# Feed-forward's first projection by seven block products in place of eight, with the sums of weight blocks made by accumulating transfers

## The chip, the cores and the metric

The kernel runs on one core of one Trainium2 chip. The metric is device time in microseconds of one execution; a lower number is better. A core has five engines with queues of their own, each worked off in order: TensorE (PE in the profile; its weight loads are PEld), VectorE (DVE), ScalarE (ACT), GpSimd (POOL) and SyncE (SP). Transfers between the chip's memory (HBM) and the core's memory (SBUF) are issued from one of these queues and carried by 16 DMA engines. TensorE writes its results into eight banks of PSUM.

## What is computed

The reference runs four layers over a sequence of 512 tokens of width 1024, all in 32-bit floats. Each layer is a mixer (an attention, a convolution module, a gated recurrence, another attention) and then a feed-forward, and every one of the four feed-forwards has the same shape:

```
def swiglu_ffn(h, w_ffn_in, w_ffn_out):
    g, u = jnp.split(h @ w_ffn_in, 2, axis=-1)
    return (jax.nn.silu(g) * u) @ w_ffn_out

def conv_ffn(x, w_up, conv_w, conv_b, w_down):
    gate, val = jnp.split(x @ w_up, 2, axis=-1)
    ...
    return (jax.nn.silu(conv) * val) @ w_down
```

`h` is 512x1024, `w_ffn_in` 1024x5632 and `w_ffn_out` 2816x1024. The first two feed-forwards are of the first kind. The last two put a causal convolution of width 3 over the gate ahead of the `silu`.

## The kernel before

**Matmuls in three passes.** Every 32-bit operand is split into a high part, rounded to the format that TensorE takes at full rate, and the low rest. ScalarE writes the high part (a copy), VectorE the low one (a subtraction). A product is then three matmuls (`mm3`): high by high, high by low, low by high. The activations lie in SBUF feature-major as `xh` and `xl`, eight blocks of 128 features by 512 tokens.

**Weights in units.** All weights are 379 units of 128x1024 (512 KB) in one tensor `wall`, in the order of use. `w_dma` loads unit after unit on SP's queue, `w_hi` (ScalarE) and `w_lo` (VectorE) split them, and `W.cur` counts the units taken by the matmuls. Loads run at most `AHEAD_DMA` = 8 units ahead of it, splits `AHEAD` = 5.

**The feed-forward.** `ffn` goes over 22 pairs of units (128 gate columns and the 128 value columns that go with them). For each unit `fm_unit` takes 8 blocks of 128 features by three matmuls of 512 columns: 24 matmuls, 48 for a pair. The first four units go by `fm_quads`, in halves of 256 columns: 256 tokens for all four units first, since the later tokens are not ready yet. `epi` follows each pair: `silu` (with the convolution in the last two feed-forwards) on the gate, the product with the value, and the split of that product into `p`. `out_proj` then takes the 22 units of the second projection, each by 8 groups of three matmuls of 512 columns, and as its results come, `boundary` runs residual, norm (whose power GpSimd takes in `rms_scale`), transposes (`xt`) and the split into `xh` and `xl` for the next stage, one block of 128 tokens (`tb`) after the other.

**Order.** A scheduler in Python (`Sched`), which runs when the program is built, sets the order of each engine's queue: tasks yield operations with an engine and an assumed cost, and the one that can start first is issued, with priorities to settle ties. That order is then fixed: an engine whose next instruction must wait holds up what stands behind it. Working memory is a pool of 34 slots of 128x1024 (`spool`), a pool of eight 128x512 tiles, and the eight PSUM banks.

## Time and profile before

| | |
|---|---|
| Three runs | 2326.4, 2327.54 and 2328.59 us; median 2327.54 |
| The profiled execution | 2326.68 us, of which the profile's span is 2324.9 |
| PE busy | 2306.1 us, 99% of the span |
| DVE, ACT, POOL busy | 1197.4 (52%), 912.1 (39%), 134.8 (6%) us |
| DMA | 224.68 MB in all, 97 GB/s on average; wall's queue 27.9% of the 16 engines |
| Granted TensorE clock | 0.998 of full speed |

The span runs from the first to the last instruction; the time of an execution is 1.78 us longer here. "Busy" of an engine is the time in which at least one of its instructions ran. Matmuls overlap in their records: each lasts longer than the distance to the next, so the distance from start to start, and not the duration, is what one costs in a stream. A granted clock of 1.00 means 2.4 GHz.

### The profile page before, as it was taken

To read this page: it belongs to the slowest core of one execution; us is meant where nothing else is said; L and a number is where in the kernel's file an instruction comes from. 1 tells how busy PE (TensorE), PEld (TensorE's weight loads), DVE (VectorE), ACT (ScalarE), POOL (GpSimd) and SP (SyncE) were. 2 spreads that over 40 slices of the span, in tenths; PEclk is the share of its full clock that TensorE was granted. 3 is DMA by queue.
4 is the path that set the end of the run, shared out by engine and by line. 5 is a ranking of instruction groups with operands and counts; after the bars stand their busy time and mean duration, and the time that the engine had idled before them with its cause. 6 is when DMAs were issued, how large, how long until landed. Compare 5 with 4: busy or idle time off the path is not lost.

```text
span 2324.9 us, 29594 instructions
## 1 busy us (share of the span) xinstructions
PE 2306.1 (99%) x11888; PEld 1969.2 (85%) x11888; DVE 1197.4 (52%) x2038; ACT 912.1 (39%) x1614; POOL 134.8 (6%) x162
## 2 busy tenths in 40 slices
PE   9999999999999999999999999999999999999998
PEld 9888988888978988888888888888888998888887
DVE  5786433333687633333564875444434655444432
ACT  6454323222466322323443444333322664333321
POOL 0000000000284000000000000000000000000000
PEclk9999999999999999999999999999999999999999
DMA  4223322233333222234121214222243022222340
GB/s 179 101 82 118 119 73 91 81 128 107 120 138 126 91 91 76 90 106 154 73 73 64 73 47 135 91 73 77 96 163 109 19 90 93 91 73 76 105 137 36
DMA packets 62936, 224.68 MB, mean 97 GB/s; under 512 B 6984, under 2 KB 7240, under 8 KB 62800
## 3 DMA queue, kind: packets, MB, share of 16 engines
q1 hardware_dynamic: 62368, 222.41, 27.9%
q8 instruction: 93, 1.52, 0.3%
q10 hardware_dynamic: 432, 0.40, 0.1%
q14 instruction: 43, 0.35, 0.0%
HBM read 220.67 MB, written 2.11 MB: 96 GB/s over the span
## 4 chain that ended last, share of the span: by engine, by line
PE 95%; POOL 1%; DVE 1%; ACT 1%; issue 1%; DMA 0%; SPq 0%; POOLq 0%; ACTq 0%
PE fm L539 18%; PE fm L540 18%; PE fm L541 18%; PE op L539 9%; PE op L541 9%; PE op L540 9%; PE tm L539 2%; PE tm L541 2%; PE tm L540 2%; POOL cy L1190 1%; PE xt L689 1%; PE O L1745 1%; PE S L1508 1%; PE o L1571 1%; PE PT L1734 1%
## 5 line engine op out<-in xcount | busy, mean ns | idle before, releaser
L539 PE MATMUL fm<-xh,wh 128*128 128x512 f32 (+1 forms) x2160 | 794.8, 368 | 0.0
L540 PE MATMUL fm<-xl,wh 128*128 128x512 f32 (+1 forms) x2160 | 787.3, 364 | 0.2 <-DVE xl L699 0.2
L541 PE MATMUL fm<-xh,wl 128*128 128x512 f32 (+1 forms) x2160 | 787.3, 364 | 0.0
L507 DVE TENSOR_TENSOR wl<-wr,wh 128x1024 fp32r<-128x1024 f32 x379 | 457.4, 1232 | 287.2 <-ACT wh L498 182.3
L498 ACT ACTIVATE wh<-wr 128x1024 fp32r<-128x1024 f32 x379 | 387.6, 1052 | 264.0 <-DMA wr<-wall 138.5
L541 PEld LDWEIGHTS fm<-xh,wl 128*128 128x128 f32 x2160 | 407.9, 189 | 65.3
L539 PEld LDWEIGHTS fm<-xh,wh 128*128 128x128 f32 x2160 | 408.3, 189 | 61.7
L540 PEld LDWEIGHTS fm<-xl,wh 128*128 128x128 f32 x2160 | 408.3, 189 | 61.4 <-DVE xl L699 0.4
L539 PE MATMUL op<-wh,p 128*128 128x512 f32 x704 | 274.9, 390 | 0.4 <-DVE sg L805 0.4
L541 PE MATMUL op<-wh,p 128*128 128x512 f32 x704 | 274.0, 389 | 0.0
L540 PE MATMUL op<-wl,p 128*128 128x512 f32 x704 | 273.9, 389 | 0.0
L805 DVE TENSOR_TENSOR sg<-fm,sg 128x512 f32<-128x512 f32 x88 | 60.9, 692 | 383.2 <-PE fm L541 376.1
L530 ACT ACTIVATE p<-sg 128x512 fp32r<-128x512 f32 x88 | 55.6, 632 | 357.4 <-DVE sg L805 357.4
L539 PEld LDWEIGHTS op<-wh,p 128*128 128x128 f32 x704 | 132.1, 188 | 28.1 <-DVE sg L805 0.9
L541 PEld LDWEIGHTS op<-wh,p 128*128 128x128 f32 x704 | 132.1, 188 | 27.7
L540 PEld LDWEIGHTS op<-wl,p 128*128 128x128 f32 x704 | 132.2, 188 | 27.0
L660 POOL TENSOR_TENSOR ss<-ss,mhalf 128x1 f32<-128x1 f32 x48 | 26.0, 541 | 1417.1 <-DVE ss L655 1417.0
L539 PE MATMUL op<-wh,y 128*128 128x512 f32 x256 | 102.7, 401 | 0.2 <-DVE y L1004 0.2
L541 PE MATMUL op<-wh,y 128*128 128x512 f32 x256 | 100.0, 391 | 0.0
L540 PE MATMUL op<-wl,y 128*128 128x512 f32 x256 | 99.8, 390 | 0.0
L531 DVE TENSOR_TENSOR p<-sg,p 128x512 fp32r<-128x512 f32 x88 | 60.9, 692 | 61.4 <-ACT p L530 61.4
L1190 POOL TENSOR_TENSOR cy<-cp,cy 128x512 f32<-128x512 f32 x60 | 86.1, 1434 | 30.2 <-ACT cp L1189 26.3
(247 smaller groups left out, 2269.9 us busy)
## 6 DMA issues: line engine op xcount, KB each, us to landing
wr<-wall SPq DMA_DIRECT2D x379, 512.0 KB, 3.6
row<-rows SPq DMA_DIRECT2D x14, 512.0 KB, 3.9
cm<-cmat SPq DMA_DIRECT2D x14, 512.0 KB, 4.0
h<-x SPq DMA_DIRECT2D x8, 256.0 KB, 6.6
nck<-negc SPq DMA_DIRECT2D x4, 512.0 KB, 5.1
alibi<-alibi SPq DMA_DIRECT2D x4, 512.0 KB, 4.4
out<-out SPq DMA_DIRECT2D x8, 256.0 KB, 2.1
mk<-masks SPq DMA_DIRECT2D x2, 288.0 KB, 5.3
```

What stands on the lines that cost most here:

```text
L498: yield act(1024, lambda: A.activation(out=b.t, in_=r.t, func=AF.Copy), (r,), (b,))
L507: yield dve(1024, lambda: V.tensor_tensor(out=b.t, in0=r.t, in1=hh.t.bitcast(F32), op=ALU.subtract), (r, hh), (b,))
L530: yield act(n, lambda: A.activation(out=y0, in_=raw, func=AF.Copy), (rb,), (yb,), psum=psum)
L531: yield dve(n, lambda: V.tensor_tensor(out=y1, in0=raw, in1=y0.bitcast(F32), op=ALU.subtract), (rb,), (yb,))
L539: T.matmul(out, lhsT=a[0], rhs=b[0], start=s, stop=False)
L540: T.matmul(out, lhsT=a[0], rhs=b[1], start=False, stop=False)
L541: T.matmul(out, lhsT=a[1], rhs=b[0], start=False, stop=e)
L660: yield Op("POOL", 0.29 + 0.167 * cols, lambda: G.tensor_tensor(out=ss[:, 8:8 + cols], in0=ss[:, 4:4 + cols], in1=mhalf[:, :cols], op=ALU. ...
L689: T.transpose(b[:, 128 * i:128 * i + 128], n[:, c:c + 128], ident)
L805: yield dve(512, lambda: V.tensor_tensor(out=c.t, in0=u.t, in1=c.t, op=ALU.mult), (u, c), (c,))
L1190: yield pool(512, lambda: G.tensor_tensor(out=y.t, in0=p.t, in1=y.t, op=ALU.add), (p,), (y,))
L1508: T.matmul(b[:, 128 * i:128 * i + 128].rearrange("p (j l) -> p j l", l=ln), lhsT=mix[:, 128 * i:128 * i + 128], rhs=dims(QP, 256 * i + ln, ...
```

## The change

The diff's core (the new `x_sums`, which spawns the sums of activations for two blocks of tokens each, the release of buffers and the passing of flags are left out):

```diff
+N_PLAIN = 2
+FFN_AT = (33, 33 + 3 * NF + 24, 33 + 6 * NF + 64, 33 + 9 * NF + 82)
+SEVEN = {u for f in FFN_AT for u in range(f + 2 * N_PLAIN, f + 2 * NF)}
+AHEAD_SEVEN = 6
...
-            yield Wait(lambda: u < W.cur + W.ahead_dma)
-            b = yield Alloc(spool, [128, 1024], F32, "wr", low=lambda: 4 if len(W.raw) > len(W.lo) + W.gone else 2)
+            yield Wait(lambda: u < W.cur + (AHEAD_SEVEN if u in SEVEN else W.ahead_dma))
+            b = yield Alloc(spool, [128, 1024], F32, "wr", low=lambda: 1 if u in SEVEN else 4 if len(W.raw) > len(W.lo) + W.gone else 2)
             yield dma(524288, lambda: nc.sync.dma_start(out=b.t, in_=ap["wall"][u]), (), (b,))
             W.raw[u] = b
+            if u in SEVEN and u % 2 != SEVEN_ODD:
+                seven_sums(u - 1)
...
+    def seven_sums(u):
+        s1, s2 = W.raw[u], W.raw[u + 1]
+        subs = []
+        def part(s):
+            x = Buf(name="wsum", need=0)
+            x.w, x.weng = s.w, "DMA"
+            subs.append((s, x))
+            return x
+        l1, r1, l2, r2 = part(s1), part(s1), part(s2), part(s2)
+        left = [3]
+        lo_, hi_ = slice(0, 512), slice(512, 1024)
+        g, v = ap["wall"][u], ap["wall"][u + 1]
+        def add(s, x, src):
+            return Op("POOL", 1.0, lambda: G.dma_start(out=s[:, lo_], in_=src, accum_op=ALU.add), (), (x,), lat=2.6)
+        def piece(name, src, x):
+            b = yield Alloc(spool, [128, 2, 512], F32R, "w" + name, need=2, low=lambda: 0 if u < W.cur + 2 else 1)
+            yield act(512, lambda: A.activation(out=b[:, 0, :], in_=src, func=AF.Copy), (x,), (b,))
+            yield dve(512, lambda: V.tensor_tensor(out=b[:, 1, :], in0=src, in1=b[:, 0, :].bitcast(F32), op=ALU.subtract), (x,), (b,))
+            W.piece[u, name] = b
...
+        def first():
+            yield from piece("11", s1[:, lo_], l1)
+            yield add(s1, l1, v[:, lo_])
+            yield from piece("t1", s1[:, lo_], l1)
+            yield add(s1, l1, v[:, hi_])
+            yield from piece("t2", s1[:, lo_], l1)
+            yield add(s1, l1, g[:, hi_])
+            yield from piece("t4", s1[:, lo_], l1)
+            end()
+        def second():
+            yield add(s2, l2, v[:, hi_])
+            yield from piece("t3", s2[:, lo_], l2)
+            yield Wait(lambda: u < W.cur)
+            yield from piece("22", s2[:, hi_], r2)
+            end()
+        def third():
+            yield Wait(lambda: u < W.cur)
+            yield from piece("21", s1[:, hi_], r1)
+            end()
+        def prio(late):
+            return lambda: -8 if u + late < W.cur + 2 else 1 + 0.001 * u
+        S.spawn(first(), prio(0), "sum1")
+        S.spawn(second(), prio(0), "sum2")
+        S.spawn(third(), prio(0), "sum3")
...
+    def keep(b, tb, kh, raws):
+        if tb not in raws:
+            raws[tb] = yield slot((128, 2, 512), F32, "xr", need=2)
+        r = raws[tb]
+        yield act(512, lambda: A.activation(out=r[:, kh, :], in_=b.t, func=AF.Copy), (b,), (r,), psum=True)
+        free(b)
...
+            yield dve(512, lambda: V.tensor_tensor(out=x.t, in0=a11, in1=a21, op=ALU.subtract), (a, b), (x,))
+            yield dve(512, lambda: V.tensor_tensor(out=a21, in0=a21, in1=a22, op=ALU.subtract), (b,), (bb,))
+            yield dve(512, lambda: V.tensor_tensor(out=a22, in0=a21, in1=a11, op=ALU.subtract), (a, bb), (bb,))
+            yield dve(512, lambda: V.tensor_tensor(out=a12, in0=a12, in1=a22, op=ALU.add), (a, bb), (ba,))
+            yield from parts(0, a21, bb)
+            yield from parts(2, x.t, x)
+            free(x)
+            yield from parts(1, a22, bb)
+            yield from parts(3, a12, ba)
...
+        def prod(b, cs, u, name, mov, rd):
+            yield Wait(lambda: (u, name) in W.piece)
+            w = W.piece.pop((u, name))
+            for k in range(4):
+                sl = slice(128 * k, 128 * k + 128)
+                yield pe(pass3(256), lambda: mm3(b[:, cs], (w[:, 0, sl], w[:, 1, sl]), mov(k), k == 0, k == 3), [w] + rd, [b])
+            free(w)
...
+        def pair(m):
+            u = at + 2 * m
+            yield Wait(lambda: (u, "11") in W.piece)
+            W.cur += 2
+            a = yield bank("fa", need=8)
+            yield from prod(a, L_, u, "11", *block(0, 0))
+            yield from prod(a, R_, u, "t1", *total(0))
+            b = yield bank("fb", need=8)
+            yield from prod(b, L_, u, "t3", *total(2))
+            yield from prod(b, R_, u, "22", *total(3))
+            d = yield bank("fd", need=4)
+            S.spawn(epi7(m, a, b, d, cs := []), -6, "epi7")
+            yield from prod(d, L_, u, "t2", *total(1))
+            c = yield bank("fc", need=8)
+            cs.append(c)
+            yield from prod(c, L_, u, "21", *block(0, 1))
+            yield from prod(c, R_, u, "t4", *block(1, 1))
...
+        def epi7(m, a, b, d, cs):
+            x = yield t2("x7", need=0)
+            v = yield t2("v7", need=0)
+            yield act(256, lambda: A.activation(out=x[:, L_], in_=a[:, L_], func=AF.Copy), (a,), (x,), psum=True)
+            yield dve(256, lambda: V.tensor_tensor(out=x[:, R_], in0=d[:, L_], in1=x[:, L_], op=ALU.add), (d, x), (x,))
+            free(d)
+            yield dve(256, lambda: V.tensor_tensor(out=v[:, L_], in0=a[:, R_], in1=x[:, R_], op=ALU.subtract), (a, x), (v,))
+            free(a)
+            yield dve(256, lambda: V.tensor_tensor(out=x[:, R_], in0=b[:, L_], in1=x[:, R_], op=ALU.add), (b, x), (x,))
+            yield dve(256, lambda: V.tensor_tensor(out=v[:, R_], in0=v[:, L_], in1=b[:, L_], op=ALU.subtract), (b, v), (v,))
+            yield dve(256, lambda: V.tensor_tensor(out=v[:, L_], in0=b[:, R_], in1=v[:, L_], op=ALU.add), (b, v), (v,))
+            free(b)
+            yield Wait(lambda: cs)
+            c = cs[0]
+            yield dve(512, lambda: V.tensor_tensor(out=x.t, in0=c.t, in1=x.t, op=ALU.add), (c, x), (x,))
+            free(c)
+            yield from epi(m, x, v)
...
-            yield dve(512, lambda: V.tensor_tensor(out=c.t, in0=u.t, in1=c.t, op=ALU.mult), (u, c), (c,))
-            free(u)
-            p = yield slot((128, 2, 512), F32R, "p", need=2)
-            spool.reserve -= 1
-            yield from split(c.t, c, (p[:, 0, :], p[:, 1, :]), p)
-            free(c)
-            ps[m] = p
...
+            yield dve(512, lambda: V.tensor_tensor(out=p[:, m % 2, :], in0=u.t, in1=c.t, op=ALU.mult), (u, c), (p,))
+            free(u, c)
+        def halves():
+            for m in range(NF):
+                yield Wait(lambda: at + 2 * NF + m < W.cur + 3 and pr.get(m // 2) is not None)
+                p = pr[m // 2]
+                y = yield slot((128, 2, 512), F32R, "ph", need=2)
+                yield from split(p[:, m % 2, :], p, (y[:, 0, :], y[:, 1, :]), y)
+                pp[m] = y
+                if m % 2:
+                    free(p)
...
+        bs = yield from fm_quads(2 * N_PLAIN)
+        for i in range(N_PLAIN):
+            S.spawn(epi(i, bs[2 * i], bs[2 * i + 1]), -5, "epi")
+        S.spawn(halves(), -5, "halves")
+        yield Wait(lambda: len(X.sums) == 4)
+        for m in range(N_PLAIN, NF):
+            yield from pair(m)
```

Twenty of the 22 pairs of each feed-forward (`SEVEN`, 80 pairs in all) are now taken as a product of 2x2 blocks: two halves of the 1024 features, two halves of the 512 tokens, and the gate and value unit. Seven products of sums of blocks (`prod`, each 4 blocks of 128 features by three matmuls of 256 columns) take the place of eight. The other two pairs go by `fm_quads` as before.

What the sums need: for the activations, `keep` copies the transposed blocks once more and `x_sums` makes four sums of 512x256, split into high and low (`xs`), once for each feed-forward. For the weights, `seven_sums` loads both units of a pair as before, and splits seven pieces of 128x512 from them: the first half of `s1`, then the same buffer after each of three additions (`t1`, `t2`, `t4`), the first half of `s2` after one (`t3`), and the two second halves. An addition (`add`) is a transfer issued from POOL's queue that reads 256 KB of `wall` a second time and adds it to what lies in SBUF. Each one waits for the split of the piece before it, which reads the same buffer.

`epi7` puts the seven results together from four PSUM banks: a copy on ScalarE and six additions on VectorE, ahead of `epi`. The split of `p` moves from `epi` to `halves`, which runs shortly before the second projection takes it. The loads of `SEVEN` units run at most 6 ahead. The scheduler's assumed cost of a matmul of n columns becomes `pass3(n)`.

The order of each engine changes with it. On PE, in the middle of the first feed-forward's first projection, six neighbouring instructions (`fm` and `fa` are PSUM banks, `wh`/`wl` a unit's high and low parts, `w11`/`wt1` pieces that hold both) stood before as follows, where one unit ends and the next begins in another bank

```order
L539 MATMUL fm_154_3300<-xh_75,wh_242_3198 128x512
L540 MATMUL fm_154_3300<-xl_76,wh_242_3198 128x512
L541 MATMUL fm_154_3300<-xh_75,wl_243_3200 128x512
L539 MATMUL fm_155_3332<-xh_75,wh_246_3234 128x512
L540 MATMUL fm_155_3332<-xl_76,wh_246_3234 128x512
L541 MATMUL fm_155_3332<-xh_75,wl_247_3236 128x512
```

and now, where one product ends and the next begins in the same bank, as

```order
L616 MATMUL fa_157_3451<-xh_75,w11_237_3109 128x256
L617 MATMUL fa_157_3451<-xl_76,w11_237_3109 128x256
L618 MATMUL fa_157_3451<-xh_75,w11_237_3109 128x256
L616 MATMUL fa_157_3451<-xs_193_2543,wt1_239_3141 128x256
L617 MATMUL fa_157_3451<-xs_194_2544,wt1_239_3141 128x256
L618 MATMUL fa_157_3451<-xs_193_2543,wt1_239_3141 128x256
```

The loads of weights are the same kind, one for each matmul; a matmul takes 256 columns in place of 512, and the second product reads sums (`xs`). A pair has 84 rows like these, and had 48.

On DVE, two pairs of the same place before (`sg` is the gate, `p` the split product, `wl` the low part of a unit):

```order
L805 TENSOR_TENSOR sg_62_3330<-fm_154_3300,sg_62_3330 128x512
L531 TENSOR_TENSOR p_258_3343<-sg_62_3330,p_258_3343 128x512
L507 TENSOR_TENSOR wl_261_3372<-wr_259_3367,wh_260_3370 128x1024
L507 TENSOR_TENSOR wl_264_3404<-wr_262_3399,wh_263_3402 128x1024
L805 TENSOR_TENSOR sg_63_3398<-fm_156_3368,sg_63_3398 128x512
L531 TENSOR_TENSOR p_265_3411<-sg_63_3398,p_265_3411 128x512
L507 TENSOR_TENSOR wl_268_3440<-wr_266_3435,wh_267_3438 128x1024
L507 TENSOR_TENSOR wl_271_3472<-wr_269_3467,wh_270_3470 128x1024
```

and one pair now (`x7` and `v7` are `epi7`'s tiles; the other rows with `w` are low parts of pieces of this pair's successors):

```order
L520 TENSOR_TENSOR wt3_293_3907<-wr_283_3765,wt3_293_3907 128x512
L520 TENSOR_TENSOR wt1_292_3892<-wr_281_3736,wt1_292_3892 128x512
L958 TENSOR_TENSOR x7_80_3908<-fd_171_3906,x7_80_3908 128x256
L520 TENSOR_TENSOR w11_294_3927<-wr_290_3862,w11_294_3927 128x512
L960 TENSOR_TENSOR v7_81_3909<-fa_169_3835,x7_80_3908 128x256
L962 TENSOR_TENSOR x7_80_3908<-fb_170_3876,x7_80_3908 128x256
L963 TENSOR_TENSOR v7_81_3909<-v7_81_3909,fb_170_3876 128x256
L520 TENSOR_TENSOR w22_297_3964<-wr_273_3620,w22_297_3964 128x512
L964 TENSOR_TENSOR v7_81_3909<-fb_170_3876,v7_81_3909 128x256
L968 TENSOR_TENSOR x7_80_3908<-fc_172_3926,x7_80_3908 128x512
L520 TENSOR_TENSOR w21_298_3982<-wr_272_3601,w21_298_3982 128x512
L997 TENSOR_TENSOR p_300_3991<-v7_81_3909,sg_82_3978 128x512
```

Between two pieces of one buffer (`wt2_295` here, and `wt1_292` before it) stands other work, and the pieces are those of pairs that PE takes two or three pairs later.

On POOL, whose queue was empty in this place, the additions now stand like this (one name of `wr` is one buffer; one row with `s1` of a pair, three in all, depend on each other, the single ones are `s2`):

```order
L515 DMA wr_235_3084<-wall 128x512
L515 DMA wr_245_3218<-wall 128x512
L515 DMA wr_235_3084<-wall 128x512
L515 DMA wr_244_3209<-wall 128x512 x2
L515 DMA wr_255_3364<-wall 128x512
L515 DMA wr_244_3209<-wall 128x512
L515 DMA wr_254_3355<-wall 128x512 x2
L515 DMA wr_265_3509<-wall 128x512
L515 DMA wr_254_3355<-wall 128x512
L515 DMA wr_264_3491<-wall 128x512 x2
L515 DMA wr_273_3620<-wall 128x512
L515 DMA wr_272_3601<-wall 128x512
```

The first addition of a pair's buffer stands behind the second or third of the pair before. In the 60 dependent additions of a feed-forward, the longest path of additions that must wait for one another, through buffers and through the queue's order, has 32, 29, 30 and 30 steps in the four feed-forwards.

## Rows read from the trace of the kernel before

**Rows 1.** The page: busy times of the engines, then the chain by line.
```profile
PE 2306.1 (99%) x11888; PEld 1969.2 (85%) x11888; DVE 1197.4 (52%) x2038; ACT 912.1 (39%) x1614; POOL 134.8 (6%) x162
...
PE 95%; POOL 1%; DVE 1%; ACT 1%; issue 1%; DMA 0%; SPq 0%; POOLq 0%; ACTq 0%
```

**Rows 2.** Timeline of PE, first projection, 512 columns: start, duration, what. 42 starts apart.
```profile
299.76 0.39 PE L539 MATMUL fm<-xh,wh 128*128 128x512 f32 x1
299.99 0.39 PE L540 MATMUL fm<-xl,wh 128*128 128x512 f32 x1
...
309.28 0.39 PE L539 MATMUL fm<-xh,wh 128*128 128x512 f32 x1
```

**Rows 3.** Timeline of PE, 256 columns: the first and last of 106 matmuls in a row.
```profile
28.05 0.28 PE L539 MATMUL fm<-xh,wh 128*128 128x256 f32 x1
28.18 0.28 PE L540 MATMUL fm<-xl,wh 128*128 128x256 f32 x1
...
40.66 0.28 PE L539 MATMUL fm<-xh,wh 128*128 128x256 f32 x1
```

**Rows 4.** Stretches inside first projections: us, busy by engine (x), PEclk, DMA share, GB/s.
```profile
270.00:470.00 200.00, 200.00 (x885) 165.58 (x884) 68.84 (x74) 57.74 (x74) 0.00 (x0) 1.00 0.25 83
1470.00:1660.00 190.00, 190.00 (x840) 157.34 (x839) 91.45 (x105) 69.56 (x88) 0.00 (x0) 1.00 0.24 82
```

**Rows 5.** The page's groups: VectorE and ScalarE operations of 512 and 1024 elements.
```profile
L507 DVE TENSOR_TENSOR wl<-wr,wh 128x1024 fp32r<-128x1024 f32 x379 | 457.4, 1232 | 287.2 <-ACT wh L498 182.3 <-PE op L540 60.9 <-PE op L541 32.1
...
L531 DVE TENSOR_TENSOR p<-sg,p 128x512 fp32r<-128x512 f32 x88 | 60.9, 692 | 61.4 <-ACT p L530 61.4
L805 DVE TENSOR_TENSOR sg<-fm,sg 128x512 f32<-128x512 f32 x88 | 60.9, 692 | 383.2 <-PE fm L541 376.1 <-ACT sg L804 7.1
...
L530 ACT ACTIVATE p<-sg 128x512 fp32r<-128x512 f32 x88 | 55.6, 632 | 357.4 <-DVE sg L805 357.4
...
L801 DVE SCALAR_TENSOR_TENSOR sg<-fm,pf,sg 128x510 f32<-128x510 f32 x44 | 33.0, 749 | 1.6
L799 DVE SCALAR_TENSOR_TENSOR sg<-fm,pf,sg 128x511 f32<-128x511 f32 x44 | 33.0, 749 | 56.5 <-ACT sg L797 56.2
...
L1552 DVE TENSOR_TENSOR QK<-QK,T 128x256 f32<-128x256 f32 x56 | 23.4, 423 | 2.4 <-PE S L1520 2.4
```

**Rows 6.** Timeline of DVE: product, its split, two weight splits one behind the other.
```profile
304.79 0.69 DVE L805 TENSOR_TENSOR sg<-fm,sg 128x512 f32<-128x512 f32 x1 [6.18 <-PE fm L541]
306.18 0.69 DVE L531 TENSOR_TENSOR p<-sg,p 128x512 fp32r<-128x512 f32 x1 [0.70 <-ACT p L530]
307.13 2.36 DVE L507 TENSOR_TENSOR wl<-wr,wh 128x1024 fp32r<-128x1024 f32 x2 [0.26 <-ACT wh L498]
```

**Rows 7.** Timeline of PE at the first feed-forward's start: last transposes, first 512-column matmul.
```profile
247.16 1.04 PE L689 MATMUL xt<-ident,nx 128*128 128x128 f32 x8
...
260.98 0.40 PE L539 MATMUL fm<-xh,wh 128*128 128x512 f32 x1
```

**Rows 8.** Transfers: source, KB each, median us from issue to landing.
```profile
wr<-wall SPq DMA_DIRECT2D x379, 512.0 KB, 3.6
...
h<-x SPq DMA_DIRECT2D x8, 256.0 KB, 6.6
...
out<-out SPq DMA_DIRECT2D x8, 256.0 KB, 2.1
```

**Rows 9.** GpSimd's addition of 128x512: nanoseconds min/median/max.
```profile
L1190 POOL TENSOR_TENSOR cy<-cp,cy x60: 1259/1294/2301, 627.5 to 722.7; 128x512 f32<-128x512 f32 x60
```

**Rows 10.** The page: GpSimd's smallest operation.
```profile
L660 POOL TENSOR_TENSOR ss<-ss,mhalf 128x1 f32<-128x1 f32 x48 | 26.0, 541 | 1417.1 <-DVE ss L655 1417.0
```

**Rows 11.** Timeline of DVE in the convolution module: one weight split.
```profile
652.56 2.05 DVE L507 TENSOR_TENSOR wl<-wr,wh 128x1024 fp32r<-128x1024 f32 x1
```

**Rows 12.** The chain of waits at that time: start us, us, what.
```profile
653.61 2.17 POOL cy L1190
```

More of the change, by code (lines that the diff above doesn't have):

```diff
@@ L485, in w_dma, with end @@
             W.raw[u] = b
+            if u in SEVEN and u % 2 != SEVEN_ODD:
+                seven_sums(u - 1)
+    SEVEN_ODD = FFN_AT[0] % 2
+    def seven_sums(u):
[17 more added lines that the diff above has]
+            W.piece[u, name] = b
+        def end():
+            left[0] -= 1
+            if left[0] == 0:
+                for s, x in subs:
+                    s.r = max(s.r, x.r)
+                    s.w = max(s.w, x.w)
+                free(s1, s2)
+                W.gone += 2
+        def first():
[22 more added lines that the diff above has]
+        S.spawn(third(), prio(0), "sum3")
@@ L535, in program @@
         blocks = None
+        sums = {}
     def mm3(out, a, b, s, e):
@@ L699, in pre_norm @@
             yield dve(512, lambda: V.tensor_tensor(out=ol, in0=src, in1=oh.bitcast(F32), op=ALU.subtract), (b,), (xb,))
-            free(b)
-    def new_blocks():
-        return [[Buf(name=f"x{tb}{kh}", need=2) for kh in range(2)] for tb in range(4)]
+            if len(blocks) > 4:
+                S.spawn(keep(b, tb, kh, blocks[4]), -9.5 + tb, "keep")
+            else:
+                free(b)
[5 more added lines that the diff above has]
+        free(b)
@@ new lines, in x_sums, with one, parts @@
+    def x_sums(raws):
+        yield Wait(lambda: 2 in raws)
+        for i in range(4):
+            X.sums[i] = ((yield slot((128, 4, 256), F32R, "xs", need=2)), (yield slot((128, 4, 256), F32R, "xs", need=2)))
+        def one(t):
+            yield Wait(lambda: t in raws and t + 2 in raws)
+            a, b = raws[t], raws[t + 2]
+            x = yield t2("xd")
+            a11, a12, a21, a22 = a[:, 0, :], a[:, 1, :], b[:, 0, :], b[:, 1, :]
+            ba, bb, ts_ = Buf(name="xa", need=0), Buf(name="xb", need=0), slice(128 * t, 128 * t + 128)
+            def parts(i, src, rd):
+                h_, l_ = X.sums[i]
+                src = src.rearrange("p (k t) -> p k t", t=128)
+                oh, ol = h_[:, :, ts_], l_[:, :, ts_]
+                yield act(512, lambda: A.activation(out=oh, in_=src, func=AF.Copy), (rd,), (h_,))
+                yield dve(512, lambda: V.tensor_tensor(out=ol, in0=src, in1=oh.bitcast(F32), op=ALU.subtract), (rd, ), (l_,))
+            yield dve(512, lambda: V.tensor_tensor(out=x.t, in0=a11, in1=a21, op=ALU.subtract), (a, b), (x,))
[7 more added lines that the diff above has]
+            yield from parts(3, a12, ba)
+            a.r = max(a.r, ba.r)
+            b.r = max(b.r, bb.r)
+            free(a, b)
+        for t in range(2):
+            S.spawn(one(t), -7, "xsum")
@@ L705, in residual, with new_blocks @@
+    def new_blocks(sums=False):
+        return [[Buf(name=f"x{tb}{kh}", need=2) for kh in range(2)] for tb in range(4)] + ([{}] if sums else [])
     def residual(tb, bs, gpost, bias):
@@ new lines, in block, with total @@
+        def block(half, kh):
+            ts_ = slice(256 * half, 256 * half + 256)
+            return (lambda k: (xh[:, 4 * kh + k, ts_], xl[:, 4 * kh + k, ts_])), [X.blocks[2 * half + i][kh] for i in range(2)]
+        def total(i):
+            a, b = X.sums[i]
+            return (lambda k: (a[:, k, :], b[:, k, :])), [a, b]
+        L_, R_ = slice(0, 256), slice(256, 512)
+        def pair(m):
[15 more added lines that the diff above has]
+            yield from prod(c, R_, u, "t4", *block(1, 1))
@@ L804, in epi @@
                 yield act(512, lambda: A.activation(out=c.t, in_=c.t, func=AF.Silu), (c,), (c,), table="silu")
-            yield dve(512, lambda: V.tensor_tensor(out=c.t, in0=u.t, in1=c.t, op=ALU.mult), (u, c), (c,))
-            free(u)
-            p = yield slot((128, 2, 512), F32R, "p", need=2)
-            spool.reserve -= 1
-            yield from split(c.t, c, (p[:, 0, :], p[:, 1, :]), p)
-            free(c)
-            ps[m] = p
-        bs = yield from fm_quads(4)
-        S.spawn(epi(0, bs[0], bs[1]), -5, "epi")
-        S.spawn(epi(1, bs[2], bs[3]), -5, "epi")
-        for m in range(2, NF):
-            g = yield from fm_unit()
-            u = yield from fm_unit()
-            S.spawn(epi(m, g, u), -5, "epi")
+            j = m // 2
+            if j not in pr:
+                pr[j] = None
+                pr[j] = yield slot((128, 2, 512), F32, "p", need=2)
+                left[0] -= 1
+                if left[0] < 1:
+                    spool.reserve -= 1
+            yield Wait(lambda: pr[j] is not None)
+            p = pr[j]
+            yield dve(512, lambda: V.tensor_tensor(out=p[:, m % 2, :], in0=u.t, in1=c.t, op=ALU.mult), (u, c), (p,))
[9 more added lines that the diff above has]
+                    free(p)
+        if len(X.blocks) > 4:
+            S.spawn(x_sums(X.blocks[4]), -7, "xsums")
+        bs = yield from fm_quads(2 * N_PLAIN)
[5 more added lines that the diff above has]
+            yield from pair(m)
+        for i in range(4):
+            free(*X.sums[i])
+        X.sums.clear()
         chain, blocks = chain_of()
-        yield from out_proj([lambda m=m: ps.get(m) for m in range(NF)], chain, R)
+        yield from out_proj([lambda m=m: pp.get(m) for m in range(NF)], chain, R)
         X.blocks = blocks
```

36 lines of the change are left out of this document (23 added, 13 removed).

## The prediction

> **What bounds the kernel now.** I read the page first: PE is busy for 2306.1 of 2324.9 us, and 95% of the chain that ended last is PE [rows 1]. So PE's queue sets the end, and a change pays if that queue gets shorter and PE does not begin to wait. Next the timeline of PE, since the records of matmuls overlap and only the distance between starts says what one costs. In a first projection 42 starts of 512-column matmuls take 309.28 - 299.76 = 9.52 us, or 0.2267 us each [rows 2]. The kernel already has 256-column matmuls of the same kind, each with a weight load of its own, in its quads: 105 starts take 40.66 - 28.05 = 12.61 us, or 0.1201 us each [rows 3]. Half the columns thus cost 53%, not 50%. Then the stretches inside the first projections, for what the other engines have free: in 200 us PE is busy throughout at a granted clock of 1.00 (its 2.4 GHz level), DVE 68.8 us, ACT 57.7 us, POOL nothing, and the DMA engines a quarter at 83 GB/s; with the convolution DVE has 91.5 of 190 us [rows 4].
>
> **The matmuls.** A pair falls from 48 matmuls of 512 columns, 48 x 0.2267 = 10.88 us, to 84 of 256 columns, 84 x 0.1201 = 10.09 us. That is 0.79 us for a pair, and 80 x 0.792 = 63.3 us for the 80 pairs. An eighth of the columns goes, but over 40% of the saving is given back, because 36 more matmuls each pay the part that does not shrink with the columns. The change's order shows 84 rows of 256 columns in a pair, so the saving on PE's queue itself is not in doubt; what is in doubt is whether PE gets its operands in time. The Trainium skill (TensorE: Matmul & The Clock Gate, Back-to-back issue gap) gives columns / 2.4 + 2.5 ns for a warm isolated stream; by that the sum would be 80 x (48 x 0.2158 - 84 x 0.1092) = 95 us, and the time about 2240 us. Rows 2 and 3 disagree: 13.4 ns are left over the columns in both, so I give that result no chance.
>
> **VectorE and ScalarE.** DVE loses two splits of 1024 elements, one product and one split for a pair, and gets seven splits of 512, five additions of 256, one of 512, and the product (the split of `p` comes later, in the second projection). By durations: 7 x 0.692 + 5 x 0.423 + 2 x 0.692 = 8.34 us, and with the convolution's two operations of 0.749 us 9.84 us [rows 5]. Two weight splits back to back take 2.36 us where their durations make 2.46 [rows 6], so 0.1 us of each overlaps its neighbour: down to 6.8 and 8.1 us. PE's 10.09 us covers that in all cases, though by only 0.25 us at the upper end with the convolution. ACT has seven copies of 0.632 us [rows 5], 4.4 us, and some two short operations: about 6 us, covered. The 22 splits moved to `halves` give the second projection 0.69 us more DVE work for each unit, which lasts 24 x 0.2267 = 5.4 us there and has one weight split of 1.23 us; I cost them at nothing, hidden by PE. If that cover were gone, 88 x 0.69 = 61 us would show.
>
> **The start of each feed-forward.** The sums of activations are new and can end only after the last block's transposes. From their end to the first matmul behind the quads PE has 260.98 - 248.20 = 12.8 us of work [rows 7]. DVE needs there, by durations, the last two activation splits 1.4 us, three weight splits 3.7, half of the sums and their splits 8 x 0.692 = 5.5, and three weight pieces 2.1: 12.7 us. It just fits, and the first additions of the weights wait in the same queues, with the norm's powers behind them on POOL. Bounds: nothing, or the 5.5 us of sums shown in full. I take 2 us, nearer to nothing since overlap shortens the 12.7; four times 2 is **8 us**.
>
> **The additions.** This has no row. Each of the four for a pair is issued by POOL, and three form a chain: addition, high split, low split, next addition. From ready data to the end of a low split rows 6 show 306.87 - 305.48 = 1.39 us; with 0.2 us for hand-overs, one step takes the addition's time T + 1.6. Bounds for T, from issue to landing: 2.1 us, as 256 KB stored, and 6.6 us, as 256 KB of `x` loaded among others [rows 8]. I take 4.5: 3.6 us as a load of 512 KB [rows 8], since an addition must also read what it adds to, and 0.9 us for POOL to issue it, between its smallest operation, 0.54 us, and an addition of its own, 1.29 us [rows 9, 10]. So a step is 6.1 us. The order's longest paths have 32 + 29 + 30 + 30 = 121 steps. The room is 4 x (20 x 10.09 + 25) = 907 us; the 25 us are the two and a half pairs by which loads run ahead. 121 x 6.1 = 738 us fits. A late addition delays what stands behind it on ACT and DVE, above all the `epi7` that frees PSUM, but a pair uses four of eight banks, so PE waits only after a whole pair's delay.
>
> The DMA engines: 83 GB/s at 0.25 [rows 4] is 332 GB/s at 1. A pair loads 1.05 MB (0.31 of 10.09 us) and adds 1.05 MB: 0.62 together if an added byte costs what a loaded one does, 0.94 if twice that.
>
> **Sum.** 2326.7 - 63.3 + 8 = 2271.4 us against the profiled execution. The median of the three runs is 0.9 us above it: **2272 us**. Its own range is 2258 (no loss at the starts, and a third of the 18.8 us in which PE idles now gone with the new order) to 2290 (5.5 us at each start).
>
> **Rivals.** *Slow additions (slower).* If T is like the 6.6 us of rows 8, a step is 8.2 us and the paths 121 x 8.2 = 992 us: 85 us more than the room, and the time 2272 + 85 = 2357 us. PE then waits for a piece in `prod`. The path fills the room at 907 / 121 = 7.5 us (T = 5.9), and the gain is used up at T = 6.4. For it: three transfers in series for every pair, the same 16 engines at 0.94 if additions count twice, and GpSimd does suffer beside DVE: one weight split took 2.05 us in place of 1.23 while GpSimd's addition took 2.17 [rows 11, 12], where its median is 1.29 [rows 9]. If issuing is stretched by that 0.9 us, T is 5.4 and still fits. Against it: the median load of twice the bytes lands in 3.6 us [rows 8], and loads here are spread over the pair. The Trainium skill (Collectives: The Full Stack, The bandwidth ceiling) says that an add in a transfer halves the rate since it reads two sources; by that 0.94 would hold. No run here shows it yet.
>
> *VectorE binds with the convolution (less gain).* Should the 17 operations of a pair wait 0.07 us each on ACT on top of 9.84 us, as the split in rows 6 does (0.70 us idle for a copy of 0.63), a pair takes 11.0 us, and 40 pairs lose 40 x 0.9 = 36 us: 2308 us. Against it: durations overlap, and other pairs' pieces stand between.
>
> *Break-even.* Waits of about 55 us, from either cause: some 2327 us.
>
> **How the numbers follow.** The forecast has 0.61, VectorE 0.10, break-even 0.04, slow additions 0.25. About 0.2% (4.7 us) is what a measurement here tells from no change. Faster by more: 0.70; within it: 0.05 (the break-even and an edge of its neighbours); slower: 0.25. The range goes from 2258 to 2360 and takes in slow additions up to the largest landing of rows 8; left out are additions slower than that, about 0.12, and 0.03 below.
>
> **What would show it.** Right: starts 0.120 us apart in `fa` to `fc`, PE busy above 98% in the stretches of the pairs, DVE 70 to 95% there, additions landing in under 5.9 us, the span near 2269. Wrong: PE idle before `prod` matmuls, released by DVE's low splits, and these in turn by ACT and by transfers; landings over 6 us or a DMA share near 1 would mean slow additions, DVE without idle time in the last two feed-forwards alone would mean the second rival, and gaps only at the first pair of each feed-forward an undersized start.

## The result, and the profile after

The changed kernel takes 2525.41 us (median of 4 runs, 2520.51 to 2528.95) where the kernel before took 2327.76 (4 runs on the same chip): a ratio of 1.0848, 95% interval 1.0827 to 1.0869. The forecast was 2272, the range 2258 to 2360. So the kernel is slower by far more than the forecast's slower case allowed. The profiled execution has a span of 2527.2 us at a granted clock of 0.968.

The page of the changed kernel: busy times, clock by slices, DMA queues (packets, MB, share of 16 engines), groups (busy, mean ns | idle before), and transfers (KB, median us from issue to landing):

```profile
PE 2338.5 (93%) x14796; PEld 2116.2 (84%) x14796; DVE 1589.0 (63%) x2982; ACT 1119.6 (44%) x2158; POOL 416.5 (16%) x482
...
PEclk9999989999999999899999999998999999998999
...
q1 hardware_dynamic: 62368, 222.41, 27.1%
q0 software_dynamic: 46080, 83.91, 20.8%
...
L520 DVE TENSOR_TENSOR wt<-wr,wt 128x512 fp32r<-128x512 f32 x320 | 219.8, 689 | 373.3 <-ACT wt L519 371.1
...
L616 PE MATMUL fb<-xs,w 128*128 128x256 f32 x320 | 104.4, 326 | 100.7 <-ACT w L519 100.5
...
wr<-wall SPq DMA_DIRECT2D x379, 512.0 KB, 4.4
wr<-wall POOLq DMA_DIRECT2D x320, 256.0 KB, 5.1
```

Against [rows 1] PE is no longer busy throughout: 2527.2 - 2338.5 = 188.7 us idle, where it was 18.8. Its busy time rose too, by 32 us, though it should have fallen by 63. The additions (`POOLq`) land in 5.1 us in the median, and the loads beside them need 4.4 us where they needed 3.6 [rows 8].

The whole of the pairs' stretch in the first feed-forward (from the first `fa` to the last `fc`) and in the third, which overlaps the convolution; columns as in [rows 4]:

```profile
264.00:525.00 261.00, 218.57 (x1680) 211.60 (x1680) 147.98 (x273) 95.66 (x177) 61.79 (x71) 0.95 0.72 154
1560.00:1817.00 257.00, 223.18 (x1686) 216.23 (x1685) 173.56 (x306) 108.98 (x194) 60.97 (x70) 0.93 0.71 153
```

20 pairs x 10.09 us would be 202 us. They take 261 and 257, and no engine is full: DVE has 57% and 68%, ACT 37% and 42%, the DMA engines 0.72. So this is no bound of an engine but of waiting. Who waits for whom (us in total, times, longest), first over the whole execution, then PE's alone:

```profile
ACT wt L519 <- DMA wr<-wall: 567.3, 205, 8.6
DVE wt L520 <- ACT wt L519: 371.1, 180, 6.5
...
PE fb L616 <- ACT w L519: 100.5, 36, 7.2
PE fb L618 <- DVE w L520: 32.3, 51, 3.0
```

The lines read as a chain. ACT's copy of a sum (`wt`) stands first in its queue and waits for the landing, 205 times out of 320 and for 567.3 us. DVE waits behind ACT for 371.1 us. And PE waits for `w` in bank `fb`: that is piece "22", which needs **no addition at all**. The timeline of ACT (start us, us, engine, line, what [idle before it <- whom it waited for]) shows how it becomes late:

```profile
407.09 0.62 ACT L519 ACTIVATE wt<-wr 128x512 fp32r<-128x512 f32 x1
410.22 0.63 ACT L519 ACTIVATE wt<-wr 128x512 fp32r<-128x512 f32 x1 [2.50 <-DMA wr<-wall]
410.76 1.66 ACT L519 ACTIVATE w<-wr 128x512 fp32r<-128x512 f32 x3
414.93 0.63 ACT L975 ACTIVATE sg<-x 128x512 f32<-128x512 f32 x1 [2.51 <-DVE x L968]
```

At 407.7 us the queue stops for 2.50 us in front of "t1" of the next pair. The three copies behind it (`w`, by the order of the queue "11" of the pair after that, then "22" and "21" of the pair that PE is on) need no addition, and follow the landing in one go of 1.66 us. PE then stands still for 1.50 us, until 413.96, in front of the low part of "22", which DVE makes behind ACT's copy (the second of the two merged into one row here; then PE's own row):

```profile
412.62 1.29 DVE L520 TENSOR_TENSOR w<-wr,w 128x512 fp32r<-128x512 f32 x2
```
```profile
413.96 0.39 PE L618 MATMUL fb<-xs,w 128*128 128x256 f32 x1 [1.50 <-DVE w L520]
```

The second cost is in the clock. PE's timeline after a wait, and the granted clock (third number from the right) of its first matmuls and of the stretch behind them:

```profile
453.26 0.39 PE L618 MATMUL fb<-xs,w 128*128 128x256 f32 x1 [2.97 <-DVE w L520]
453.48 0.28 PE L616 MATMUL fb<-xs,w 128*128 128x256 f32 x1
453.60 0.28 PE L617 MATMUL fb<-xs,w 128*128 128x256 f32 x1
...
454.93 0.42 PE L618 MATMUL fd<-xs,wt 128*128 128x256 f32 x1
455.14 0.41 PE L616 MATMUL fd<-xs,wt 128*128 128x256 f32 x1
455.36 0.41 PE L617 MATMUL fd<-xs,wt 128*128 128x256 f32 x1
```
```profile
453.20:453.50 0.30, 0.24 (x2) 0.24 (x3) 0.14 (x2) 0.13 (x1) 0.00 (x0) 1.00 0.84 143
454.80:457.40 2.60, 2.60 (x14) 2.60 (x13) 1.95 (x4) 1.94 (x4) 0.34 (x1) 0.50 0.01 1
```

The granted clock is 0.50 from 454.80 us on, the 1.2 GHz level, though PE has worked again since 453.26 us; before that it had stood still for 2.97 us. Starts are 0.213 us apart there in place of 0.120. In the four first projections 574 of 6720 distances between starts lie between 0.20 and 0.26 us; without the additions (below) none does. 468 of them lie in stretches with a granted clock of 0.50, and some 44 us are lost by these (468 x 0.093) while PE counts as busy. The other 106 lie at a clock of 1.00, 94 of them right behind a wait, as from 453.26 to 453.48 us above; they make another 11 us.

### The profile page after: what moved, and what is told of

The parts are those of the page before. It is cut to its first block, busy times and chain, and to the rows that moved or that the text cites. A ratio compares the mean times of both kernels' runs of the same rounds, so it can differ in the third digit from the quotient of the medians.

```text
span 2527.2 us, 38133 instructions
## 1 busy us (share of the span) xinstructions
PE 2338.5 (93%) x14796; PEld 2116.2 (84%) x14796; DVE 1589.0 (63%) x2982; ACT 1119.6 (44%) x2158; POOL 416.5 (16%) x482
## 3 DMA queue, kind: packets, MB, share of 16 engines
q0 software_dynamic: 46080, 83.91, 20.8%
## 5 line engine op out<-in xcount | busy, mean ns | idle before, releaser
L519 ACT ACTIVATE wt<-wr 128x512 fp32r<-128x512 f32 x320 | 198.5, 627 | 584.5 <-DMA wr<-wall 567.3
L515 POOL DMA_DIRECT2D wr<-wall x320 | 279.2, 952 | 1075.1 <-DVE wt L520 596.3
L520 DVE TENSOR_TENSOR wt<-wr,wt 128x512 fp32r<-128x512 f32 x320 | 219.8, 689 | 373.3 <-ACT wt L519 371.1
L616 PE MATMUL fm<-xh,wh 128*128 128x256 f32 (+1 forms) x880 | 297.6, 338 | 0.0
L617 PE MATMUL fm<-xl,wh 128*128 128x256 f32 (+1 forms) x880 | 289.2, 329 | 0.4 <-DVE xl L779 0.4
L618 PE MATMUL fm<-xh,wl 128*128 128x256 f32 (+1 forms) x880 | 289.3, 329 | 0.0
L616 PE MATMUL op<-wh,ph 128*128 128x512 f32 x704 | 276.4, 393 | 5.0 <-DVE x L958 3.6
L618 PE MATMUL op<-wh,ph 128*128 128x512 f32 x704 | 274.9, 391 | 0.0
L617 PE MATMUL op<-wl,ph 128*128 128x512 f32 x704 | 274.9, 391 | 0.0
L616 PE MATMUL fb<-xs,w 128*128 128x256 f32 x320 | 104.4, 326 | 100.7 <-ACT w L519 100.5
L618 PEld LDWEIGHTS fm<-xh,wl 128*128 128x128 f32 x880 | 167.5, 190 | 15.4
L617 PEld LDWEIGHTS fm<-xl,wh 128*128 128x128 f32 x880 | 168.0, 191 | 11.9 <-DVE xl L779 0.8
L616 PEld LDWEIGHTS fm<-xh,wh 128*128 128x128 f32 x880 | 168.0, 191 | 11.0
L616 PEld LDWEIGHTS op<-wh,ph 128*128 128x128 f32 x704 | 132.8, 189 | 34.3 <-DVE x L958 4.4
L618 PEld LDWEIGHTS op<-wh,ph 128*128 128x128 f32 x704 | 132.7, 189 | 27.8
L617 PEld LDWEIGHTS op<-wl,ph 128*128 128x128 f32 x704 | 132.8, 189 | 27.2
L618 PE MATMUL fb<-xs,w 128*128 128x256 f32 x320 | 108.1, 338 | 32.5 <-DVE w L520 32.3
```

Source lines behind the costliest of these rows:

```text
L515: return Op("POOL", 1.0, lambda: G.dma_start(out=s[:, lo_], in_=src, accum_op=ALU.add), (), (x,), lat=2.6)
L519: yield act(512, lambda: A.activation(out=b[:, 0, :], in_=src, func=AF.Copy), (x,), (b,))
L520: yield dve(512, lambda: V.tensor_tensor(out=b[:, 1, :], in0=src, in1=b[:, 0, :].bitcast(F32), op=ALU.subtract), (x,), (b,))
L616: T.matmul(out, lhsT=a[0], rhs=b[0], start=s, stop=False)
L617: T.matmul(out, lhsT=a[0], rhs=b[1], start=False, stop=False)
L618: T.matmul(out, lhsT=a[1], rhs=b[0], start=False, stop=e)
```

## The experiments

Times of single runs stand beside the kernel before on the same chips, 2325.95 to 2328.34 us in all of them.

**1. Without the additions.** The order of all other instructions stays.

```diff
-            return Op("POOL", 1.0, lambda: G.dma_start(out=s[:, lo_], in_=src, accum_op=ALU.add), (), (x,), lat=2.6)
+            return Op("POOL", 1.0, lambda: None, (), (x,), lat=2.6)
```

> Leaves out the 320 additions; the order of all other instructions stays, so the pieces t1, t2, t3 and t4 hold unsummed weights. Both A and B: all of the loss comes from the additions, and the time is what the prediction took for the matmuls and the starts, 2264-2290 us. Theory C (the new block products or the activation sums cost PE more than 0.120 us per matmul and 2 us per start, or DVE binds): above 2310 us.

Measured: 2273.84 us. The page, and the two stretches of the pairs:

```profile
PE 2249.9 (99%) x14796; PEld 2061.4 (91%) x14796; DVE 1579.2 (70%) x2982; ACT 1109.8 (49%) x2158; POOL 137.9 (6%) x162
```
```profile
263.00:465.00 202.00, 202.00 (x1684) 201.98 (x1684) 146.46 (x273) 92.40 (x174) 0.00 (x0) 1.00 0.33 101
1434.00:1636.00 202.00, 202.00 (x1685) 202.00 (x1685) 173.46 (x310) 106.22 (x194) 0.00 (x0) 1.00 0.32 100
```

202 us at a clock of 1.00, with the convolution or without, and a time within the range of theories A and B. All that is lost, 2527.2 - 2272.1 = 255.1 us of span, comes from the additions: PE's idle time rose from 22.2 to 188.7 us (166.5), its busy time from 2249.9 to 2338.5 (88.6).

**2. The same bytes, not accumulated.** What was loaded last then stands in place of the sums; queue, order and sizes stay.

```diff
-            return Op("POOL", 1.0, lambda: G.dma_start(out=s[:, lo_], in_=src, accum_op=ALU.add), (), (x,), lat=2.6)
+            return Op("POOL", 1.0, lambda: G.dma_start(out=s[:, lo_], in_=src), (), (x,), lat=2.6)
```

> The additions become plain transfers of the same 256 KB to the same place from the same queue, in the same order (the sums are replaced by what was last loaded). If reading what is added to is what makes a landing slow, the median landing falls from 5.1 us to about 3.5 and the DMA share of the POOL queue from 20.8% to about 10%, and the time to 2350-2450 us. If issuing from POOL and the fixed part make it, landings stay at 4.5-5.5 us and the time at 2480-2540 us.

Measured: 2341.82 us. Queue, issue on POOL and landing:

```profile
q0 software_dynamic: 25600, 83.91, 10.8%
...
L515 POOL DMA_DIRECT2D wr<-wall x320 | 172.6, 541 | 992.4 <-DVE wt L520 518.5
...
wr<-wall POOLq DMA_DIRECT2D x320, 256.0 KB, 3.3
```

That is 8 us below the range expected for this case. Accumulating costs 184 us here. For the same 83.91 MB it makes 46080 packets of 25600, takes 20.8% of the engines' time in place of 10.8%, and lands in 5.1 us in place of 3.3. But even plain transfers, whose median is below the 3.6 us that the scheduler assumes, lose 68 us against none: 125 of the 320 land later than 3.6 us, a tenth later than 5.1, and ACT still waits 351.8 us for landings.

**3. Only the assumed duration of an addition.** The scheduler writes the queues by it; no instruction is added or taken away but filler matmuls (`warm`), which it puts on PE where its own plan leaves PE waiting. Three kernels, 5.1, 6.5 and 8.5 us in all from issue to landing (3.6 in the changed kernel):

```diff
-            return Op("POOL", 1.0, lambda: G.dma_start(out=s[:, lo_], in_=src, accum_op=ALU.add), (), (x,), lat=2.6)
+            return Op("POOL", 0.9, lambda: G.dma_start(out=s[:, lo_], in_=src, accum_op=ALU.add), (), (x,), lat=4.2)
```

(and `lat=5.6`, `lat=7.6`.)

> Only the scheduler's assumption on an addition changes: 0.9 us of issue and 4.2 us to landing (5.1, the median of the changed kernel's trace) in place of 1.0 and 2.6. The same instructions stand in another order. Theory A (queue order: PE waits since the split of a just-in-time piece, 22 above all, stands in ScalarE's queue behind a split that waits for an addition which lands later than the scheduler thought): PE's idle time ahead of the 22 product falls from 133 us to below 60, the time to 2300-2430 us. Theory B (the three additions of a pair are too slow one after the other, whatever stands between them): the time stays within 2480-2560 us.

> As e1, with 6.5 us to landing assumed in place of 5.1 (the measured median is 5.1 to 5.6, the ninth decile 7.7): the order alone changes. If what is left in e1 is made by the additions that land later than assumed, the time falls to 2340-2385 us. If the chain itself is too long, it stays within 2385-2440 us, since no order shortens it.

> The changed kernel with all its additions as transfers, and again only the assumed duration changed: 8.5 us in all from issue to landing (3.6 in the changed kernel, 5.1 and 6.5 in the two runs that gave 2403.7 and 2361.5). That is above nine in ten of the landings of the 6.5 us run (the ninth decile there is 8.1 us). Theory A (nearly all that is left of the loss is order): ACT's waits for a landing fall from 297.6 us to under 150, the time to 2305 to 2345, and the two first projections without the convolution come near the 208 us that the mixed sums gave. Theory B (what is left is the shared transfer engines: the queue's landings grow as the pairs come closer together, whatever the order): landings of over 6 us in the median, 2350 or more.

Measured: 2403.72, 2361.49 and 2378.79 us. The filler matmuls of the changed kernel, then of the kernels with 6.5 and 8.5 us (each from its own groups):

```profile
L2085 PE MATMUL warm<-zeros 128*128 128x128 f32 x220 | 28.6, 286 | 1.0 <-POOL zeros L2090 1.0
```
```profile
L2085 PE MATMUL warm<-zeros 128*128 128x128 f32 x576 | 72.0, 283 | 1.0 <-POOL zeros L2090 1.0
```
```profile
L2085 PE MATMUL warm<-zeros 128*128 128x128 f32 x1052 | 126.8, 278 | 1.0 <-POOL zeros L2090 1.0
```

| assumed us | time us | median landing | ACT's wait for landings | filler matmuls |
|---|---|---|---|---|
| 3.6 | 2525.41 | 5.1 | 567.3 | 220 |
| 5.1 | 2403.72 | 5.6 | 386.0 | 232 |
| 6.5 | 2361.49 | 5.7 | 297.6 | 576 |
| 8.5 | 2378.79 | 6.0 | 169.3 | 1052 |

This is the main finding. The order alone is worth 164 us, with landings that are no faster. PE's waits ahead of "22" fall from 132.8 us (100.5 and 32.3 above) to 47.6 with 5.1 us:

```profile
PE fb L616 <- ACT w L519: 41.7, 19, 5.8
PE fb L618 <- DVE w L520: 5.9, 21, 0.3
```

The chain theory, by which no order helps, fails in both of the first two runs. At 5.1 us the plan still hides the additions (12 more fillers, 3 us). At 6.5 us it doesn't: the plan itself makes PE wait, 72.0 - 28.6 = 43 us. At 8.5 us PE waits for hardly a piece any more (3.2 us at most for any one group), but the plan holds 126.8 - 28.6 = 98 us of filler, and 2272.1 + 98.2 is within 7 us of the span of 2376.9. So the length of the additions isn't free either: with the best of the four orders 88 us remain over the kernel without additions, and none of them beats the kernel before. Of the two theories for the last kernel neither came true as it was put: the landings did reach 6.0 us and the time passed 2350, but the loss is planned waiting, not a full set of DMA engines (share 0.79 between 256 and 480 us).

**4. The two pieces that need no addition, one pair earlier.**

```diff
-            yield Wait(lambda: u < W.cur)
+            yield Wait(lambda: u < W.cur + 2)
             yield from piece("22", s2[:, hi_], r2)
...
-            yield Wait(lambda: u < W.cur)
+            yield Wait(lambda: u < W.cur + 2)
             yield from piece("21", s1[:, hi_], r1)
```

> The pieces 22 and 21 may be split one pair earlier (when the pair before starts, not when their own does). Theory A: PE's idle time ahead of the 22 product falls from 133 us to below 40 and the time to 2350-2450 us. Theory B: PE waits for t1, t2 or t4 instead, and the time stays within 2480-2560 us.

Measured: 2526.57 us, no change. PE's waits only went to other pieces:

```profile
PE fc L616 <- ACT wt L519: 53.7, 27, 3.6
PE fd L616 <- ACT wt L519: 25.2, 12, 4.2
PE fb L616 <- ACT w L519: 21.0, 10, 4.8
PE fa L616 <- DVE x L958: 19.4, 14, 7.2
```

In the last line PE waits for a bank that `epi7` (L958) frees late, the one wait that the prediction had feared. So "22" was the piece on which the delay showed, not its cause: all pieces come out of one late queue.

**5. The sums on other engines.** The pair's units are both in SBUF, so an engine can add them: all four on GpSimd; the first on VectorE and three by transfer; or three on GpSimd and the single one by transfer. The helper, and the choice ("P", "V", "D") in the first of the three:

```diff
+                return Op("POOL", 1.29, lambda: G.tensor_tensor(out=s[:, lo_], in0=s[:, lo_], in1=src[0], op=ALU.add), (sb, x), (x,))
...
-            yield add(s1, l1, v[:, lo_])
+            yield add(s1, l1, (s2[:, lo_], v[:, lo_]), l2, "P")
```

> All four sums of a pair are made by GpSimd's own additions from the two loaded units, in place of accumulating transfers; the second reading of the weights goes, the chain of three stays. Landing (chain) theory: a step falls from about 7 us to 1.3 to 2.2 us of addition plus 1.6, so PE hardly waits and the time is 2270-2300 us. Rival (VectorE and GpSimd get into each other's way): GpSimd is busy 5.2 us or more of each 10.1 us beside a VectorE at 74 to 85%, additions take over 2 us each, VectorE has no idle time, and the time is above 2330 us.

> The first sum (t1) is made by VectorE (0.69 us), the other three by accumulating transfers as before, with the 5.1 us to landing of e1 assumed. The chain has two transfers in place of three. If the length of the chain makes what e1 left (2404 us), the time falls to 2285-2340 us. If it is the traffic or the order, with three transfers of four left, the time falls by a quarter of e1's excess at most: 2365-2410 us.

> The three dependent sums on GpSimd, the independent one (t3) as an accumulating transfer. The transfer is then in no chain: the time is that of the kernel with all four on GpSimd, within 12 us. If a single transfer that lands late holds up a split in ScalarE's queue and with it all behind it, the time is more than 12 us above it.

Measured: 2402.36, 2379.99 and 2353.97 us. The first kernel comes out as the rival had it, though its additions take 1.3 and 1.6 us in the median and not over 2. The second kernel has two transfers in its chain in place of three. It is 24 us faster than the one with three and the same assumed 5.1 us, which was 130 us behind the kernel without additions: less than a quarter comes back, so the chain's length is not what makes most of the rest. Now the split of a sum, and GpSimd's additions (ns min/median/max for those of two buffers, and of two halves of one buffer) with all four on GpSimd; then the third feed-forward's pairs in that kernel:

```profile
L526 DVE TENSOR_TENSOR wt<-wr,wt 128x512 fp32r<-128x512 f32 x320 | 294.5, 924 | 87.7 <-ACT wt L525 82.2
...
L518 POOL TENSOR_TENSOR wr<-wr,wr x160: 1262/1296/1786, 213.3 to 2255.0; 128x512 f32<-128x512 f32 x160
L518 POOL TENSOR_TENSOR wr<-wr x160: 1262/1616/2277, 214.7 to 2261.1; 128x512 f32<-128x512 f32 x160
```
```profile
1484.00:1724.00 240.00, 219.43 (x1689) 214.25 (x1688) 222.60 (x312) 114.22 (x199) 104.05 (x71) 0.95 0.27 87
```

VectorE's split of a sum takes 924 ns on average in place of 689, and half of GpSimd's additions 1616 in the median in place of 1294 [rows 9]; the other half is no slower. They are in each other's way, as [rows 11, 12] had shown once: of all 560 splits, the 231 that lie beside a GpSimd addition for 30% of their time or more take 1.20 us on average, the other 329 take 0.68. The Trainium skill (SBUF — State Buffer, "SBUF: two separate sides") has VectorE operations with two SBUF inputs share a port pair with GpSimd, the one blocking the other, if GpSimd reads SBUF too; the trace agrees. With the convolution VectorE is then busy for 222.60 of 240 us, more than the 202 us that PE needs. One addition in four moved back to a transfer gave 48 us, where at most 12 had been expected. With so few of them the accumulating transfers land in 3.8 us, and VectorE's split of a sum falls to 786 ns; which of the two gave how much was not taken apart.

**6. Order or load, in the mixed kernel.** Assumed durations again, now 2.0 us for a GpSimd addition (1.29) and 5.4 for the transfer (5.1).

> The kernel of the run before (three dependent sums on GpSimd, the fourth by an accumulating transfer), with only the durations changed that the scheduler assumes when it writes the queues: 2.0 us for a GpSimd addition (1.29 assumed, about 1.4 measured) and 5.4 us for the transfer (3.8 measured); no instruction is added or removed. Theory A (what is lost is the order's optimism: pieces that PE needs next stand in ACT's and VectorE's queues behind splits whose sum is not there yet): some of the 80 us that separate 2354.0 from 2272 come back, 2330 to 2346, and ACT's waits for sums shrink. Theory B (what is lost is load: VectorE at over 0.9 of the two feed-forwards that overlap the convolution): within 6 us of 2354, with those two first projections still 227 us each.

Measured: 2331.48 us. Stretches of the pairs, without and with the convolution:

```profile
264.00:471.00 207.00, 203.32 (x1675) 202.42 (x1674) 178.07 (x274) 98.20 (x180) 93.55 (x72) 0.99 0.46 120
1446.00:1668.00 222.00, 207.93 (x1683) 204.19 (x1682) 206.31 (x310) 110.37 (x195) 94.81 (x70) 0.99 0.42 109
```

Without the convolution the pairs came down from 211 to 207 us (and to 202 in the second feed-forward), so what had been lost there was order. With it they came down from 227 to 222. There VectorE alone is busy for 206.31 us, more than 202, and no order can hide that; but that accounts for 4 of the 20 us that are left, and what makes the other 16 is not shown.

**7. Seven products only where VectorE has room.** These are the first two feed-forwards; the others go back to eight products. With the assumed durations of 6, and with those of the earlier mixed kernel:

```diff
-SEVEN = {u for f in FFN_AT for u in range(f + 2 * N_PLAIN, f + 2 * NF)}
+SEVEN = {u for f in FFN_AT[:2] for u in range(f + 2 * N_PLAIN, f + 2 * NF)}
```

> The same sums as in the run beside this one, assumed durations too, but seven products only in the first two feed-forwards; the last two, which overlap the convolution, go back to eight products. Arithmetic from the run with the mixed sums: there the first two first-projection stages took 210.8 us each, against 201.8 us without any addition and about 217.6 us for eight products (201.8 plus a quarter of the 63.3 us of matmuls), the last two 227.0 us each. With the last two at 217.6 us: 2352.2 - 2 x 9.4 = 2333 us of span, less what the second projections of those two lose, about 10 us: 2318 to 2336. Theory A (order) puts it at the low end, 2312 to 2322, faster than before; theory B (load) puts it at 2324 to 2336, no better than before.

> As the run beside this one, seven products in the first two feed-forwards only, but with the durations assumed as in the earlier mixed run (1.29 us for a GpSimd addition, 5.1 us for the transfer). Theory A (order): 2322 to 2332, some 5 to 12 us above its neighbour. Theory B (load): within 3 us of its neighbour.

Measured: 2317.69 us (5 runs, 2316.21 to 2318.24) against 2327.06 (14 runs), ratio 0.9960, interval 0.9945 to 0.9974; and 2328.18 us (10 runs), ratio 1.0006, 0.9996 to 1.0015. The second feed-forward's pairs in the first of them:

```profile
810.00:1012.00 202.00, 202.00 (x1685) 201.94 (x1684) 172.93 (x272) 93.86 (x173) 96.25 (x73) 1.00 0.45 120
```

PE is full again, and this version beats the kernel before by 0.4%, the only one here that does. The same instructions under a more optimistic plan are 10.5 us slower and gain nothing. Both came out as the theory of order had it.

## Why the prediction was wrong

**Right: the matmuls.** The 0.1201 us of a 256-column matmul [rows 3] held: 20 pairs take 202 us without the additions. VectorE is then busy for 7.3 us of a pair, with the convolution 8.7, within the bounds given.

**Luck: the sum.** -63.3 and +8 us gave 2272, and without the additions the kernel takes 2273.84; but the 8 us are not at the starts. The first start in that kernel, from the end of the last transposes to the first `fa`:

```profile
249.94:263.18 13.24, 13.24 (x111) 13.20 (x111) 13.10 (x22) 10.85 (x19) 0.00 (x0) 1.00 0.39 119
```

PE works throughout, for 13.2 us where it had 12.8 [rows 7], and VectorE's 13.10 us just fit, as was forecast. At all four starts together PE idles for 0.2 us. Some 11 us were added outside the feed-forwards, 5 of them between the first and the second, where the sum had no term. So one term that was too large and one that was missing nearly cancel. Two slips of the prediction change nothing: VectorE has 16 operations a pair with the convolution, not 17, which makes its lower bounds 6.9 and 8.2 us; and 5.5 us at each start would give 2286, not 2290.

**The size of T: off, but not by enough.** It was taken as 4.5 us from issue to landing; the median is 5.1, a tenth lie over 7.6. By the prediction's own sum 121 x (5.1 + 1.6) = 811 us still fit the room of 907, and the rival "slow additions", which needs T above 5.9, would not have come into force. The point at which the path fills was even about right: a plan with 5.1 us fits, one with 6.5 us doesn't.

**The step that failed** is the sentence behind that sum: "A late addition delays what stands behind it on ACT and DVE [...] but a pair uses four of eight banks, so PE waits only after a whole pair's delay." The delay on ACT and DVE was seen, but put at nothing, with PSUM banks as PE's only cover. PE also waits for pieces. Each addition that lands later than the plan assumed stops everything behind it in ACT's queue, ready or not: other pairs' sums, `epi7`, and the pieces "22" and "21", which the plan makes just before PE takes them (`yield Wait(lambda: u < W.cur)`). The rows of DVE's queue shown with the change have both, `w22_297` and `w21_298`; they belong to the very next pair, and not, as the text there says of all pieces, to one that PE takes two or three pairs later. What counts is not whether T fits the room, but whether it fits the 3.6 us **with which the order was written**. 316 of the 320 landings came later than 3.6 us, and ACT stood still in front of 205. The diff showed the number (`1.0`, `lat=2.6`); my T stood 0.9 us above it, and I did not follow that. The runs with other assumed durations show it: 122 us back with 5.1 us, 164 with 6.5. The sign named for being wrong, PE idle before `prod`, released by DVE's splits, these by ACT and by transfers, is just what came.

**A term that was missing:** the clock. With the waits come stretches at the 1.2 GHz level, of which the pairs have none without the additions; the prediction priced waits at their length alone. 88.6 of the 255.1 us are PE's busy time; by their starts some 44 of them are matmuls at the lower level, and 11 mostly first matmuls behind a wait. The rest was not taken apart; each wait also leaves the last matmul's full record (0.28 us) uncovered.

**The rivals.** An added byte does cost the DMA engines twice a loaded one (20.8% against 10.8%), as the rival took it. The Trainium skill (Collectives: The Full Stack, The bandwidth ceiling) has the same for a collective's add, and the trace agrees. But the 0.94 of that sum was for a pair in 10.09 us, and at 261 / 20 = 13.05 us it makes 0.73, where 0.72 was measured: the engines were not full. "VectorE binds with the convolution" did not show in the changed kernel (DVE 68%), but VectorE is at 93% there once GpSimd makes all the sums (222.60 of 240 us).

**What stays open:** how much of the landings' growth (3.8 to 4.3 us when one sum in four is a transfer, 5.1 to 6.0 when all are) comes from the loads and how much from other additions. Not tried: a deeper look-ahead, which would need more buffers.

## What to carry to other kernels

Where a program fixes the order of its queues by assumed durations, compare each assumption with the duration you expect on the chip, tail included, before any argument about room: an operation that is later than assumed holds up ready work behind it. Here a duration near the late landings (6.5 us) did better than the median (5.1) and than one so long (8.5) that the plan itself waits; try several. And a wait on TensorE can cost more than its length.

## What was not expected of the hardware

An accumulating transfer of 256 KB made 144 packets for 80 of a plain one and doubled the engines' time; POOL's record of its issue is 0.95 us on average against 0.54 us. It lands in 3.8 to 4.3 us with one for each pair, and in 5.1 to 6.0 us with four. A split on VectorE takes 0.68 us alone and 1.20 us on average beside GpSimd's additions of the same size.
